# A Strassen-style feed-forward opening put in written order, and one more product beside each table operation of the last state-space quarter

## The chip, the cores and the metric

One core of a Trainium2 chip. The kernel is one launch; its time is the device time of that launch in microseconds (us), here the median of three runs. Engines are called by the profile's names: PE (TensorE products; PEld its weight loads), DVE (VectorE), ACT (ScalarE), POOL (GpSimd) and SP (the engine that issues nearly all DMAs).

## The reference, cut to what matters

One layer of a decoder trunk on x of 1024 tokens by 1024 channels, all in float32:

```python
h = rms_norm(x, mix_norm_g)                      # one projection of h feeds three mixers
y_ssm, y_conv, y_attn = s5(...), short_conv(...), sparse_attention(...)
mixed = sum_b sigmoid(gate_b) * y_b
x = x + mixed @ w_out
h = rms_norm(x, ffn_norm_g)
x = x + (silu(h @ w_gate) * (h @ w_up)) @ w_down   # inner width 2816
```

The s5 mixer is a diagonal complex state-space layer. The kernel computes it in four quarters of its groups.

## The kernel before, in words

Every float32 product is made of three PE products of split operands: each operand x is split into hi (written by ACT, a copy rounded to fp32r) and lo = x - hi (written by DVE, `split`, lines 59 to 62), and hi*hi, hi*lo and lo*hi are added up in PSUM. "A product" below is one of these PE instructions, 128x128 weights by 512 columns; a group that belongs together has 12 of them (4 blocks of the inner dimension by 3).

PSUM has four one-bank accumulators (`acc`) and two two-bank ones (`wide`); SBUF is cut into 44 pages of 128x1024 and 14 half pages. The framework's planner orders the instructions of each engine by the order of the program text and by when it believes operands to be ready; on the chip each engine then runs its list in that order. Within `manual_schedule(engines=...)` the listed engines keep the order of the text among the instructions of that block; what is written before or after the block may still be placed between them.

**State-space quarters.** `s5` loops over q = 0..3 (PE in written order). In each pass the table operations on DVE (`s5_scan` for quarter q, then `s5_tables` for quarter q+1, 25 steps) are followed by `beat()`, which takes a number `F5B` of products from a generator of other work, the filler (`tail`: the rest of the convolution, then the products of two mixers, `mix_plain`). Every 12 products of `mix_plain` end in one DVE instruction (L1166) that empties an accumulator. What is left of the filler after quarter 3 is run by `drain`, then `mix_ssm` follows, whose inputs are the quarters' outputs (`s5_out`, which ends in ACT's L1075, then `s5_back` through memory, then `s5_parts`, a split); its first 12 products end in ACT's L1192.

**The output projection and the feed-forward opening.** `out_rows` computes x + mixed @ w_out by a seven-product Strassen scheme (order `OUT`), 28 steps of four token blocks. The last four steps (p = 4, i = 0..3, the steps 24 to 27) add to the same four accumulators `first[0..3]` that p = 7 has filled; `into` (L1292, DVE) adds an accumulator to a row block of x. `row` normalises a finished block: a sum of squares on ACT (`square_sum`, L219), a square root on ACT (L209), a reciprocal (L210) and a scaling (L215 on DVE or L213 on ACT). `quadrants` transposes normalised blocks on PE, 128x128 at a time (L1373), in fours into a half of a `wide`, from which ACT (L1379) or, for the differences T1, DVE (L1377) takes them; `operand_b` splits them. Of the eight row blocks, 0 to 3 make `half0` (quadrants 11 and 21), 4 to 7 make `half1` (T1 and 22); T2, T3 and T4 are differences made by DVE (L1389).

`ffn_up` is a generator: it fetches weights, makes operands A (`operand`), and then runs groups of 12 products (here called items) in the order of the list `flat`, each preceded by the operand of the item three later. Items 0 to 11 are p = 1 and p = 2 for i = 0..2 and z = 0 (gate), 1 (up); p = 2 adds to the accumulator of p = 1 after ACT has copied it (`p1`, L1520). Items from 12 on need T1, T2, T3, T4 and 22, and for many of them a sum S made by DVE (L1449) before the split. Each `next(up)` in `out_rows` runs the generator to its next `yield`. In the kernel before all engines of this part are ordered by the planner.

Of the kernel before, what the change touches and what calls it, by code (L numbers as in the profile page):

```python
# [11 lines left out]
AF = mybir.ActivationFunctionType  # L12
# [3 lines left out]
P = 128  # L16
# [3 lines left out]
KD = D // P  # L20
# [13 lines left out]
class Trunk:  # L34
# [1069 lines left out]
    def s5(self):  # L1104
        self.yT = []
        tab = self.tab
        for q in range(4):
            bp, cr, bb, ep = tab.pop(q)
            M = self.s5_kernel(q, cr, bb)
            cp = self.s5_carry(cr)  # L1110
            U = self.U[q]
            B = self.s5_inputs(q, bp)
            if q:
                self.s5_back()
            self.F5B = 3.5 if q < 3 else 5
            X = self.s5_scan(q, U, B, ep)
            if q < 3:
                for _ in self.s5_tables(q + 1, tab):
                    self.beat()
            self.fill(self.F5S)  # L1120
            self.s5_out(q, U, M, X, cp)
        self.fill(16)
        self.s5_back()
        self.fill(16)
        self.s5_parts()
# [130 lines left out]
    def out_rows(self):  # L1256
        nc = self.nc
        v = nc.vector
        x2, ss, xn = {}, self.const("ss2", [P, NT]), {}
        self.spill_x = self.dram.tile([S, D], F32, tag="sx", name="sx")  # L1260
        up = self.ffn_up()
        seq, parts = self.out_seq, {}

        def load(t):
            x2[t] = self.page("x2")
            nc.sync.dma_start(x2[t], self.i["x"][0, t * P:(t + 1) * P, :])

        def split(n):
            if n >= len(seq) or n in parts:
                return  # L1270
            p, i = seq[n]
            if n not in self.out_parts:
                self.out_right(n)
            r = self.left[i]
            if p in (1, 2):
                t = r.pop(p)
            else:
                t = self.page("lp", F32R)
                self.split(t[:, :512], t[:, 512:], r["src"].pop(p))
            parts[n] = t, self.out_parts.pop(n)  # L1280

        def mm(ps, n, t):
            p, i = seq[n]
            act, w = parts[n]
            for j, (x, y) in enumerate(((0, 0), (0, 1), (1, 0))):
                nc.tensor.matmul(ps, act[:, x * 512 + t * P:x * 512 + (t + 1) * P], w[:, y * 512:y * 512 + 512],  # L1286
                                 start=i == 0 and j == 0 and p in (1, 5, 2), stop=i == 3 and j == 2,
                                 skip_group_check=True)

        def into(t, c, ps):  # L1290
            o = x2[t][:, c * 512:c * 512 + 512]
            v.scalar_tensor_tensor(o, ps, 0.5, o, op0=OP.mult, op1=OP.add)  # L1292

        def row(t, act):
            self.square_sum(x2[t], ss[:, t:t + 1])
            xn[t] = self.norm_row(x2[t], ss[:, t:t + 1], act)
            nc.sync.dma_start(self.spill_x[t * P:(t + 1) * P, :], x2[t])
            del x2[t]
        INTO = {1: ((0, 0),), 2: ((0, 0),), 5: ((1, 1),), 6: ((0, 1),), 3: ((0, 1),), 7: ((1, 1),), 4: ((1, 0),)}
        for t in range(4):  # L1300
            load(t)
        first = [self.acc() for _ in range(4)]
        second = None
        for n, (p, i) in enumerate(seq[:-4]):
            if i == 0 and p in (5, 2):
                second = []
                for _ in range(2):
                    a = self.wide()
                    second += [a[:, :512], a[:, 512:]]
            if p == 2:  # L1310
                load(4 + i)
            for m in range(n, n + 3):
                split(m)
            for t in range(4):
                ps = (first if p in (1, 6, 7) else second)[t]
                mm(ps, n, t)
                if i == 3:
                    for h, c in INTO[p]:
                        into(4 * h + t, c, ps)
            del parts[n]  # L1320
            if p == 7 and i < 2:
                row(2 * i, 0)
                row(2 * i + 1, 0)
            if p == 7 and i == 0:
                next(up)
        n0 = len(seq) - 4
        for n in range(n0, n0 + 4):
            split(n)
        self.B, half0 = {}, [xn.pop(j) for j in range(4)]
        q = self.quadrants(half0, 0)  # L1330
        for t in range(4):
            for n in range(n0, n0 + 4):
                mm(first[t], n, t)
            into(4 + t, 0, first[t])
            if t == 0:
                q += self.quadrants(half0, 4)
            elif t == 1:
                self.operand_b("11", q[:4])
                next(up)
            elif t == 2:  # L1340
                self.operand_b("21", q[4:])
            if t:
                row(3 + t, t % 2)
        row(7, 0)
        parts.clear()
        next(up)
        half1 = [xn.pop(4 + j) for j in range(4)]
        b11, b21 = q[:4], q[4:]
        t1 = self.quadrants(half1, 0, b11)
        self.operand_b("T1", t1)  # L1350
        next(up)
        b22 = self.quadrants(half1, 4)
        t2 = self.difference(v, b22, t1)
        self.operand_b("T2", t2)
        next(up)
        t3 = self.difference(v, t2, b11)
        self.operand_b("T3", t3)
        next(up)
        t4 = self.difference(v, b21, t2)
        self.operand_b("T4", t4)  # L1360
        self.operand_b("22", b22)
        self.run(up)

    def quadrants(self, xs, k0, less=None):

        nc = self.nc
        r = []
        for k in range(k0, k0 + 4):
            if k % 2 == 0:
                page, two = self.page("bq"), self.wide()  # L1370
            b = two[:, (k % 2) * 512:(k % 2) * 512 + 512]
            for j in range(4):
                nc.tensor.transpose(b[:, j * P:(j + 1) * P], xs[j][:, k * P:(k + 1) * P], self.ident)  # L1373
            o = page[:, (k % 2) * 512:(k % 2) * 512 + 512]
            g = self.gn[:, 8 + k:9 + k]
            if less:
                nc.vector.scalar_tensor_tensor(o, b, g, less[k - k0], op0=OP.mult, op1=OP.subtract)  # L1377
            else:
                nc.scalar.activation(o, b, AF.Identity, scale=g)  # L1379
            r.append(o)  # L1380
        return r

    def difference(self, eng, a, b):
        r = []
# [6 lines left out]
        return r  # L1391

    def operand_b(self, name, src):
        r = []
        for x in src:
            p = self.page("B", F32R)
            self.split(p[:, :512], p[:, 512:], x)
            r.append(p)
        self.B[name] = r


    ORDER = (1, 5, 2, 6, 7, 4, 3)
# [2 lines left out]
    def ffn_up(self):  # L1405
# [3 lines left out]
        gu = self.i["ffn_w_gate_up"][0]  # L1409
        self.spill_a = {p: self.dram.tile([D_FF // 2, HALF], F32, tag=f"sa{p}", name=f"sa{p}") for p in self.ORDER}  # L1410
        N = 3
        flat = [(i, z, p) for i in range(N) for z in range(2) for p in (1, 2)]
        flat += [(i, z, p) for i in range(N) for p in self.ORDER[1:] if p != 2 for z in range(2)]
        flat += [(i, z, p) for i in range(N, NF // 2) for z in range(2) for p in self.ORDER]
        groups = [(i, z, 0) for i in range(N) for z in range(2)]
# [15 lines left out]
        def operand(n):  # L1431
            if n >= len(flat) or flat[n] in ops:
                return
            i, z, p = flat[n]
            g = i, z, int(i >= N or i > 0 and p not in (1, 2))
            if g[2] == 0 and p == 2 and i < N - 2:
                fetch(groups.index(g) + 4)
            elif p == 5:
                fetch(max(groups.index(g) + 2, 2 * N + z))
            lo, hi = raw[g]  # L1440
            a11, a21, a12, a22 = lo[:, :, 0], lo[:, :, 1], hi[:, :, 0], hi[:, :, 1]
            cut = lambda x: x.rearrange("p (k c) -> p k c", k=4)
            if p in (1, 2, 4):
                src = {1: a11, 2: a12, 4: a22}[p]
            else:
                src = cut(self.half("S"))
                x, y, op = {5: (a21, a22, OP.add), 6: (sums.get((i, z, 5)), a11, OP.subtract),
                            7: (a11, a21, OP.subtract), 3: (a12, sums.get((i, z, 6)), OP.subtract)}[p]
                v.tensor_tensor(src, x, y, op=op)  # L1449
                if p in (5, 6):  # L1450
                    sums[i, z, p] = src
            t = self.page("A", F32R)
            self.split(cut(t[:, :512]), cut(t[:, 512:]), src)
            ops[flat[n]] = t
# [33 lines left out]
        yield  # L1488
        for n in range(5):
            operand(n)  # L1490
        yield
        for n, (i, z, p) in enumerate(flat):
            if n in (5, 7, 9, 12):
                yield
            if n == len(flat) - 5:
                self.down = self.ffn_down()
# [290 lines left out]
```

## Time and profile before

| | us |
|---|---|
| median of 3 runs (1753.19 to 1754.08) | 1753.66 |
| profiled execution, its own time | 1753.43 |
| its span in the trace | 1751.5 |
| PE busy in the span | 1728.9 |
| DVE busy | 1202.8 |
| ACT busy | 795.4 |

Busy PE time contains modelled ends of overlapping products, so a gap is read from the start of one product to the start of the next.

### The profile page before, as it was taken

What the parts mean: (1) busy time and instruction counts of PE and PEld (TensorE: products, weight loads), DVE (VectorE), ACT (ScalarE), POOL (GpSimd) and SP (SyncE); (2) the same over time, 40 slices, a digit from 0 to 9 for tenths busy, and PEclk for the clock granted to TensorE, in tenths of its full rate; (3) what the DMA queues carried; (4) which work ended last, traced back from release to release, by engine and by line L of the source; (5) the groups of instructions that cost most, each with busy time, mean ns of one, the idle gap of its engine ahead of it and who ended that gap; (6) DMA issues with size and microseconds to landing.
All of it is one profiled execution on the core that took longest, in us unless ns stands there. A gap on an engine that the chain in (4) does not pass through costs nothing.

```text
span 1751.5 us, 23611 instructions
## 1 busy us (share of the span) xinstructions
PE 1728.9 (99%) x8637; PEld 1433.2 (82%) x8637; DVE 1202.8 (69%) x2414; ACT 795.4 (45%) x1477; POOL 108.8 (6%) x94
## 2 busy tenths in 40 slices
PE   8999999999999999999999999999999999999999
PEld 8987788888888888888788888778888888888887
DVE  6975456667676664684685687798677776687681
ACT  7415566777777842333122244742222332344460
POOL 0000000000000010121000000011122111120000
PEclk9999999999999999999999999999999999999999
DMA  5213422221211125123566224333223332577521
GB/s 173 73 43 101 125 85 67 61 61 46 58 43 47 42 81 145 41 69 97 191 200 200 84 96 133 120 127 127 96 96 109 114 103 78 189 256 259 163 91 48
DMA packets 172664, 189.78 MB, mean 108 GB/s; under 512 B 16937, under 2 KB 129669, under 8 KB 172549
## 3 DMA queue, kind: packets, MB, share of 16 engines
q1 hardware_dynamic: 172517, 188.27, 33.5%
q8 instruction: 68, 1.11, 0.3%
q14 instruction: 47, 0.39, 0.1%
q10 hardware_dynamic: 32, 0.01, 0.0%
HBM read 134.50 MB, written 47.45 MB: 104 GB/s over the span
## 4 chain that ended last, share of the span: by engine, by line
PE 86%; DVE 6%; ACT 4%; issue 1%; DMA 1%; SPq 1%; POOL 0%; POOLq 0%; ACTq 0%; DVEq 0%
PE wide L1517 13%; PE acc L124 12%; PE acc L120 12%; PE acc L122 11%; PE acc L1517 9%; PE acc L1624 6%; PE wide L1624 5%; PE acc L560 3%; PE wide L519 3%; PE acc L1286 2%; PE wide L1286 2%; PE acc L583 2%; PE acc L582 2%; PE wide L257 1%; PE wide L256 1%
## 5 line engine op out<-in xcount | busy, mean ns | idle before, releaser
L120 PE MATMUL acc<-hh,whi 128*128 128x512 f32 x672 | 268.6, 400 | 1.5 <-DVE kl L66 1.5
L122 PE MATMUL acc<-hl,whi 128*128 128x512 f32 x672 | 267.9, 399 | 0.0
L124 PE MATMUL acc<-hh,wlo 128*128 128x512 f32 x672 | 267.4, 398 | 0.0
L1517 PE MATMUL wide<-B,A 128*128 128x512 f32 x1056 | 250.6, 391 | 0.3
L1517 PEld LDWEIGHTS wide<-B,A 128*128 128x128 f32 x1056 | 196.5, 188 | 47.0 <-DVE sg L1530 3.3
L1517 PE MATMUL acc<-B,A 128*128 128x512 f32 x792 | 190.6, 391 | 2.6 <-ACT A L61 1.6
L1517 PEld LDWEIGHTS acc<-B,A 128*128 128x128 f32 x792 | 147.9, 188 | 35.4 <-ACT A L61 2.5
L120 PEld LDWEIGHTS acc<-hh,whi 128*128 128x128 f32 x672 | 126.6, 188 | 22.3 <-issue 2.2
L122 PEld LDWEIGHTS acc<-hl,whi 128*128 128x128 f32 x672 | 126.7, 188 | 19.7 <-issue 0.2
L124 PEld LDWEIGHTS acc<-hh,wlo 128*128 128x128 f32 x672 | 126.8, 189 | 19.4 <-DVE wlo L62 0.4
L61 ACT ACTIVATE A<-S 128x512 fp32r<-128x512 f32 x88 | 54.8, 627 | 164.9 <-DVE S L1449 164.3
L62 DVE TENSOR_TENSOR ptl<-acc,pth 128x512 fp32r<-128x512 f32 (+1 forms) x152 | 93.8, 619 | 50.4 <-ACT pth L61 49.2
L1624 PE MATMUL acc<-wdp,act 128*128 128x512 f32 x528 | 121.5, 389 | 0.1
L524 DVE CUSTOM_DVE_ANT_0 p<-wide,mask 128x640 f32<-128x640 f32 (+7 forms) x128 | 90.1, 704 | 43.2 <-PE wide L519 40.5
L62 DVE TENSOR_TENSOR wlo<-raw,whi 128x1024 fp32r<-128x1024 f32 (+1 forms) x75 | 90.4, 1209 | 39.5 <-ACT whi L61 23.9
L1624 PEld LDWEIGHTS acc<-wdp,act 128*128 128x128 f32 x528 | 99.0, 188 | 21.2 <-DVE wdp L62 0.5
L1473 POOL TENSOR_TENSOR sg<-sg 128x512 f32<-128x512 f32 x44 | 73.9, 1679 | 590.3 <-ACT A L61 512.5
L527 ACT ACTIVATE p<-p,small 128x640 f32<-128x640 f32 (+7 forms) x128 | 93.6, 731 | 37.1 <-DVE small L524 35.1
L120 PE MATMUL acc<-mhi,whi 128*128 128x512 f32 x256 | 100.5, 392 | 1.8 <-DVE m L1166 1.8
L61 ACT ACTIVATE pth<-acc 128x512 fp32r<-128x512 f32 (+1 forms) x152 | 80.9, 534 | 46.0 <-PE acc L560 45.2
L124 PE MATMUL acc<-mhi,wlo 128*128 128x512 f32 x256 | 100.7, 393 | 0.3 <-DVE wlo L62 0.3
L122 PE MATMUL acc<-mlo,whi 128*128 128x512 f32 x256 | 100.5, 393 | 0.0
(397 smaller groups left out, 3246.1 us busy)
## 6 DMA issues: line engine op xcount, KB each, us to landing
raw<-in_ffn_w_gate_up_dram SPq DMA_DIRECT2D x52, 512.0 KB
raw<-in_w_in_dram SPq DMA_DIRECT2D x48, 512.0 KB
sa<-sg SPq DMA_DIRECT2D x77, 256.0 KB
araw<-sa SPq DMA_DIRECT2D x77, 256.0 KB
sg<-tg SPq DMA_DIRECT2D x48, 256.0 KB
gp<-sg SPq DMA_DIRECT2D x24, 512.0 KB
x<-in_x_dram SPq DMA_DIRECT2D x16, 512.0 KB
wd<-in_ffn_w_down_dram SPq DMA_DIRECT2D x11, 512.0 KB
```

The lines of the kernel that those rows point to most:

```text
L61: self.nc.scalar.activation(hi, src, AF.Copy)
L62: self.nc.vector.tensor_tensor(lo, src, hi.bitcast(F32), op=OP.subtract)
L120: self.nc.tensor.matmul(out, hi(k), mh(k), start=start and j == 0, stop=False)
L122: self.nc.tensor.matmul(out, hi(k), ml(k), start=False, stop=False)
L124: self.nc.tensor.matmul(out, lo(k), mh(k), start=False, stop=stop and j == n - 1)
L519: nc.tensor.matmul(ps[:, c * 512:c * 512 + w], self.QS[t][:, h], k[:, k0 + c * w:k0 + c * w + w], start=z == 0, stop=z == 1)
L524: nc.vector.tensor_tensor_reduce(p[:, :n].rearrange("p (c w) -> p c w", c=pieces), v, m.rearrange("p (c w) -> p c w", c=pieces), scale=-1. ...
L527: nc.scalar.activation(p[:, :n], p[:, :n], AF.Exp, scale=-1.0, bias=st[:, hh:hh + 1], accum_out=st[:, 2 + hh:3 + hh])
L1286: nc.tensor.matmul(ps, act[:, x * 512 + t * P:x * 512 + (t + 1) * P], w[:, y * 512:y * 512 + 512], start=i == 0 and j == 0 and p in (1, 5, ...
L1473: e.tensor_tensor(o, x, y, op=op)
L1517: nc.tensor.matmul(ps, x, y, start=p in (1, 5, 6, 7) and k + j == 0, stop=k == 3 and j == 2, skip_group_check=True)
L1624: nc.tensor.matmul(ps, act[:, x * 512 + t * P:x * 512 + (t + 1) * P], w[:, y * 512:y * 512 + 512], start=i == 0 and j == 0 and p in (1, 5, ...
```

## The change

In `s5` the 25 steps of `s5_tables` for the last quarter (made in the pass q = 2) take 4.5 products each in place of 3.5. In `out_rows` everything from the last four steps of the output projection to the split of quadrant 22 stands in one block in which PE, DVE and ACT keep the written order; the transposes of half0 stand among the products of the last four steps, four per step; the sums of squares of blocks 5 and 7 go from ACT to DVE; `quadrants` becomes `flip` (one k at a time, same instructions); the transposes of half1 stand in pairs between items 5 to 8. In `ffn_up` the first 12 items run z innermost, so that p = 2 no longer follows directly on its p = 1, and the generator yields more often.

```diff
             if q < 3:
+                self.F5B = 3.5 if q < 2 else 4.5
                 for _ in self.s5_tables(q + 1, tab):
                     self.beat()
...
-        def row(t, act):
-            self.square_sum(x2[t], ss[:, t:t + 1])
+        def row(t, act, dve=False):
+            if dve:
+                v.tensor_tensor_reduce(self.page("junk"), x2[t], x2[t], scale=1.0, scalar=0.0, op0=OP.mult, op1=OP.add,
+                                       accum_out=ss[:, t:t + 1])
+            else:
+                self.square_sum(x2[t], ss[:, t:t + 1])
...
+        with self.tc.manual_schedule(engines={E.PE, E.DVE, E.Activation}):
+            for s in range(16):
+                t = s // 4
+                mm(first[t], n0 + s % 4, t)
+                if 2 <= s < KD + 2:
+                    self.flip(half0, s - 2, b0)
+                if 3 <= s < KD + 3:
+                    self.operand_b("11" if s < 7 else "21", b0[s - 3:s - 2])
+                if s % 4 == 3:
+                    into(4 + t, 0, first[t])
+                if s in (7, 10, 14):
+                    next(up)
+                elif s == 11:
+                    row(4, 1)
+                elif s == 12:
+                    row(5, 0, True)
+                elif s == 13:
+                    row(6, 0)
+            row(7, 0, True)
+            parts.clear()
+            next(up)
+            next(up)
+            half1 = [xn.pop(4 + j) for j in range(4)]
+            for k in range(4):
+                self.flip(half1, k, b1, b0[k])
+                if k % 2:
+                    next(up)
+            b11, b21, t1 = b0[:4], b0[4:], b1[:4]
+            self.operand_b("T1", t1)
+            for k in range(4, KD):
+                self.flip(half1, k, b1)
+                if k % 2:
+                    next(up)
+            b22 = b1[4:]
+            t2 = self.difference(v, b22, t1)
+            self.operand_b("T2", t2)
+            t3 = self.difference(v, t2, b11)
+            next(up)
+            self.operand_b("T3", t3)
+            t4 = self.difference(v, b21, t2)
+            next(up)
+            self.operand_b("T4", t4)
+            self.operand_b("22", b22)
         self.run(up)
...
-        flat = [(i, z, p) for i in range(N) for z in range(2) for p in (1, 2)]
+        flat = [(i, z, p) for i in range(N) for p in (1, 2) for z in range(2)]
...
         for n in range(5):
             operand(n)
+            if n in (0, 1, 2):
+                yield
         yield
         for n, (i, z, p) in enumerate(flat):
-            if n in (5, 7, 9, 12):
+            if n in (5, 6, 7, 8, 9, 10, 12):
                 yield
```

## Rows read from the trace of the kernel before

**Rows 1.** The page, part 1: busy us (share) and instructions of each engine.

```profile
PE 1728.9 (99%) x8637; PEld 1433.2 (82%) x8637; DVE 1202.8 (69%) x2414; ACT 795.4 (45%) x1477; POOL 108.8 (6%) x94
```

**Rows 2.** Windows: stretch, length, busy of PE, PEld, DVE, ACT, POOL, clock, DMA.

```profile
848.00:857.00 9.00, 9.00 (x39) 7.38 (x38) 8.25 (x19) 0.88 (x1) 0.46 (x1) 0.83 1.00 376
...
1075.00:1104.60 29.60, 29.50 (x143) 23.40 (x142) 21.11 (x36) 22.80 (x42) 0.00 (x0) 1.00 0.80 272
1104.60:1121.70 17.10, 14.91 (x69) 12.00 (x68) 7.08 (x14) 12.46 (x23) 0.00 (x0) 1.00 0.43 146
1121.70:1157.60 35.90, 34.24 (x156) 26.70 (x157) 35.25 (x59) 23.69 (x43) 0.00 (x0) 1.00 0.24 81
1157.60:1240.00 82.40, 82.40 (x365) 68.08 (x364) 71.11 (x94) 24.64 (x41) 19.04 (x12) 1.00 0.36 123
```

**Rows 3.** Timeline of PE, 843 to 852 us: start, us, instruction [idle before <-releaser].

```profile
844.34 0.39 PE L124 MATMUL acc<-mhi,wlo 128*128 128x512 f32 x1
846.53 0.47 PE L120 MATMUL acc<-mhi,whi 128*128 128x512 f32 x1 [1.81 <-DVE m L1166]
...
847.86 0.63 PE L124 MATMUL acc<-mhi,wlo 128*128 128x512 f32 x1
...
850.84 0.50 PE L120 MATMUL acc<-mhi,whi 128*128 128x512 f32 x1
```

**Rows 4.** Timeline of DVE, 832 to 856 us.

```profile
843.06 0.68 DVE L903 TENSOR_TENSOR tt<-lpi,bbi 128x512 f32<-128x512 f32 x1
843.66 1.22 DVE L62 TENSOR_TENSOR wlo<-raw,whi 128x1024 fp32r<-128x1024 f32 x1
...
845.71 0.68 DVE L1166 SCALAR_TENSOR_TENSOR m<-gp,acc 128x512 f32<-128x512 f32 x1
```

**Rows 5.** Timeline of ACT, 895 to 965 us.

```profile
910.54 1.03 ACT L1075 ACTIVATE YN<-wide 128x1024 f32<-128x1024 f32 x1 [18.87 <-PE wide L1072]
...
923.27 2.07 ACT L61 ACTIVATE mhi<-yT 128x1024 fp32r<-128x1024 f32 x1 [10.76 <-DMA yT<-sy]
...
939.34 0.60 ACT L1192 ACTIVATE tgp<-acc 128x512 f32<-128x512 f32 x1 [12.11 <-PE acc L124]
```

**Rows 6.** Timeline of PE, 1085 to 1123 us.

```profile
1086.82 3.00 PE L1286 MATMUL acc<-wop,lp 128*128 128x512 f32 x12
...
1104.65 13.77 PE L1517 MATMUL acc<-B,A 128*128 128x512 f32 x60
1118.26 0.81 PE L1373 MATMUL wide<-ident,xn 128*128 128x128 f32 x6
1120.27 0.44 PE L1373 MATMUL wide<-ident,xn 128*128 128x128 f32 x2 [1.20 <-DVE xn L215]
1121.71 1.49 PE L1517 MATMUL acc<-B,A 128*128 128x512 f32 x5 [1.00 <-ACT A L61]
```

**Rows 7.** Timeline of DVE, 1083 to 1100 us.

```profile
1087.80 0.69 DVE L1292 SCALAR_TENSOR_TENSOR x<-acc,x 128x512 f32<-128x512 f32 x1 [3.23 <-PE acc L1286]
...
1088.60 0.75 DVE L215 TENSOR_SCALAR xn<-x,ss 128x1024 f32<-128x1024 f32 x1
...
1091.68 1.88 DVE L1292 SCALAR_TENSOR_TENSOR x<-acc,x 128x512 f32<-128x512 f32 x3
...
1095.28 0.68 DVE L62 TENSOR_TENSOR lp<-tgp,lp 128x512 fp32r<-128x512 f32 x1
```

**Rows 8.** Timeline of ACT, 1079 to 1165 us.

```profile
1079.72 1.05 ACT L219 ACTIVATE junk<-x 128x1024 f32<-128x1024 f32 x1
...
1080.89 0.29 ACT L209 ACTIVATE ss<-ss,eps 128x1 f32<-128x1 f32 x1
...
1109.63 2.18 ACT L61 ACTIVATE B<-bq 128x512 fp32r<-128x512 f32 x4
```

**Rows 9.** The page, part 5: one of the costliest groups, count | busy, mean ns.

```profile
L62 DVE TENSOR_TENSOR wlo<-raw,whi 128x1024 fp32r<-128x1024 f32 (+1 forms) x75 | 90.4, 1209 | 39.5 <-ACT whi L61 23.9
```

**Rows 10.** Timeline of PE, 1136 to 1162 us.

```profile
1142.27 3.01 PE L1517 MATMUL acc<-B,A 128*128 128x512 f32 x12 [0.69 <-ACT p L1520]
```

More of the change, by code (lines that the diff above doesn't have):

```diff
@@ L1329, in out_rows @@
         self.B, half0 = {}, [xn.pop(j) for j in range(4)]
[L1330 to L1359, printed above, removed]
@@ L1360, in out_rows @@
-        self.operand_b("T4", t4)
-        self.operand_b("22", b22)
+        b0, b1 = [], []
+        E = mybir.EngineType
+        with self.tc.manual_schedule(engines={E.PE, E.DVE, E.Activation}):
[41 more added lines that the diff above has]
+            self.operand_b("22", b22)
@@ L1362, in out_rows, with flip @@
         self.run(up)
-    def quadrants(self, xs, k0, less=None):
+    def flip(self, xs, k, r, less=None):
         nc = self.nc
[L1367 to L1381, printed above, removed]
+        if k % 2 == 0:
+            self.flip_page, self.flip_ps = self.page("bq"), self.wide()
+        w = slice((k % 2) * 512, (k % 2) * 512 + 512)
+        b, o, g = self.flip_ps[:, w], self.flip_page[:, w], self.gn[:, 8 + k:9 + k]
+        for j in range(4):
+            nc.tensor.transpose(b[:, j * P:(j + 1) * P], xs[j][:, k * P:(k + 1) * P], self.ident)
+        if less is not None:
+            nc.vector.scalar_tensor_tensor(o, b, g, less, op0=OP.mult, op1=OP.subtract)
+        else:
+            nc.scalar.activation(o, b, AF.Identity, scale=g)
+        r.append(o)
@@ L1393, in operand_b @@
     def operand_b(self, name, src):
-        r = []
         for x in src:
@@ L1397, in operand_b @@
             self.split(p[:, :512], p[:, 512:], x)
-            r.append(p)
-        self.B[name] = r
+            self.B.setdefault(name, []).append(p)
     ORDER = (1, 5, 2, 6, 7, 4, 3)
```

## The prediction

> **What bounds the kernel now.** I read the shares of busy time first: PE 99% [rows 1]. So a change can only win what PE still waits, and loses whatever new wait it puts on PE. Then the windows, for where PE has gaps: none from 1157.6 to 1240 us (82.40 of 82.40), but 2.2 us in 1104.6 to 1121.7 and 1.7 us in 1121.7 to 1157.6, with DVE at 35.25 of 35.90 there [rows 2]. Last the timelines of PE around both edits, for what ends each gap. "Busy" hides small waits, so I count by starts: one product costs (13.77 - 0.39) / 59 = 0.227 us, one transpose (0.81 - 0.27) / 5 = 0.11 us, 0.27 being what a lone transpose takes to its end [rows 6]. From 1121.71 to item 16 (1157.67, just past the window's end) PE ran 156 instructions, items 5 to 15 (132 products, 29.96) and 24 transposes (2.62): 32.6 us of work in 36.0, so 3.4 us of waits [rows 2, 6]. From item 4's end (1104.65 + 60 x 0.227 = 1118.26) to 1121.71 stand 8 transposes (0.87) and 2.6 us of waits, on the scaling of block 7 and on an ACT split [rows 6].
>
> **The state-space edit.** A step from 844.34 to 846.53 us is a wait of 2.19 - 0.23 = 1.96 us: the 49th product of the mixer needs an accumulator that DVE's L1166 has yet to empty, and L1166 stands behind table operations that are dependent and always ready [rows 3, 4]. After it the granted clock falls: 0.83 on average from 848 to 857 [rows 2], and from 847.86 to 850.84 there are seven steps of 0.426 [rows 3], the lower level, 1.2 GHz; with the one before them, eight products lose 0.2 each, 1.6 us. With 4.5 products a step, the mixer starts and its 13th product comes two to three table steps earlier in the text, so L1166 can follow the eighth table operation, which starts at 843.06 and is over at 843.66 by the pitch of its neighbours [rows 4]. If the 1.22 us weight split still goes ahead, L1166 starts at 844.8 and PE waits till 845.6, 1.0 us; if not, it starts at 843.66 and PE waits nothing. I take 0.5 us left and full clock: 1.96 + 1.6 - 0.5 = 3.1 us won. Bounds: 3.6, and nothing if DVE keeps its order. The 25 x 1 = 25 products come out of what is left after the last quarter (5.7 us). The cover there: from L1075 (910.54) the outputs are split on ACT by 923.27 + 2.07 and on DVE 2.1 later, 927.4; they are needed from the tenth product of a group of 12 that ends at 939.3, so at 938.6 [rows 5]. 11.2 us of cover become 5.5. Cost nothing; 1 us if DVE's backlog eats it. The weights and gate pages that these products ask SP for come up to 5.7 us sooner, into a stretch with a DMA share of 1.00 [rows 2]; each is fetched two or three uses ahead, so I take nothing, and the same 1 us as its bound.
>
> **Opening, stage 1: the last four projection steps.** In the text PE now does all four steps for block 0 first, then block 1. Steps 26 and 27 need splits written ahead of the block, so the planner places them as before: behind four L1292 and the norm of block 3, in a DVE queue that starts with the L1292 that waited 3.23 us for PE (1087.80) and ends with the last lo at 1095.28 + 0.68 = 1095.96 [rows 7]. The four transposes that ran ahead of p = 7's last step go behind: 0.44 less, 1095.5. Before, PE went round this by taking other blocks and transposes. Now step 27's last product for block 0 cannot start before 1095.5, though PE is free for these four steps, 3.2 us of work with the first transposes, from 1086.82 - 0.44 + 12 x 0.227 = 1089.1 on [rows 6]. Left from 1095.5: 37 products (8.4) and 28 transposes (3.1), so item 0 starts at 1107.0 in place of 1104.65: **+2.4**. Bounds: 0, if the planner moves these splits into DVE's 3.2 us hole, and 2.5.
>
> **Stage 2: items 0 to 4.** These are 60 products, 1107.0 to 1120.6 if nothing waits; blocks 4 to 7 are then long normalised, so the 2.6 us of waits before 1121.71 go. What is late next: item 2 adds to item 0's accumulator, which ACT must have copied. PE comes to it at 1107.0 + 24 x 0.227 = 1112.4. ACT's queue ahead of that copy, in written order: the evacuations and splits of half0, paced by PE, whose last transposes end at 1102.9 (behind these ACT still has one evacuation, two splits of B and two of operands, 2.7 with the pitch below and a handover of 0.2 to 0.3: 1105.9), then block 4's sum of squares and root, 1080.89 + 0.29 - 1079.72 = 1.46 [rows 8], to 1107.3; its reciprocal with two handovers, 0.3; block 5's sum on DVE, an operation that the trace before doesn't have: the nearest row, an elementwise one of 1024 columns, is 1.21 [rows 9], I take 1.25 (bounds 0.6, the pitch of a 512-column one, and 1.8, three of these), 1108.9; root 0.35; block 6's sum and root 1.46, 1110.7; reciprocal and scaling 0.3 + 0.75 [rows 7], 1111.8; item 2's lo and the last L1292 on DVE, 0.6 each, the pitch (1.88 - 0.69) / 2 of [rows 7], 1113.0; block 7's sum 1.25, root 0.45, 1114.7; two splits at (2.18 - 0.62) / 3 = 0.52 [rows 8], 1115.7; the copy 0.6: 1116.3. PE waits **3.9 us**. Then 36 products and 8 transposes: item 5 starts at 1125.4 against 1121.71, +3.7 in all. On SP, the x blocks' writes and the weight fetches for i = 2 (four DMAs, asked for with the operands of items 2 and 3, by 1116) move too; the first split of those weights is item 8's, past 1125: hidden, and 1 us if SP holds them back.
>
> **Stage 3: items 5 to 15.** PE ends items 5 to 7 and the 24 transposes at 1125.4 + 8.2 + 2.6 = 1136.2; ACT's evacuations and split, then DVE's lo for item 11, end at 1138.7. In written order DVE then makes T2's differences, T2's lo and T3's differences, 12 x 0.6, to 1146.0; only then item 12's sum (0.6). ACT's split of it and, behind that, the copy of item 9's accumulator, end at 1147.8. Item 11 needs that copy and PE is there at 1136.2 + 3 x 2.72 = 1144.3: **3.5 us**. In the trace before, such a copy held PE 0.69 once [rows 10]. Items 11 and 12 then run to 1153.2; item 13's sum stands behind T3's lo and T4's differences (1153.2), sum and split 1.3: 1.3 us and 0.3 for its lo. Item 15's sum, written after the block, comes behind T4's lo at 1160.3, or behind 22's too: 1.7 us, or 4. Together 6.8 against 3.4 before: +3.4 (bounds 0, if sums float into gaps of DVE's chain, and +5.7). Item 16 starts 3.7 + 3.4 = **7.1 us later** than before; from there PE has no waits to make it up with [rows 2].
>
> **The clock.** After the 1.96 us gap the clock fell [rows 3]; after 1.20 and 1.00 us close together it stayed at 1.00 [rows 2, 6]. A gap of 3.9 us is nearer the first, so I count one fall in stage 2, 1.6 us; in stage 3 much of it would lie in the wait for item 13. The Trainium skill (TensorE: Matmul & The Clock Gate, section "What's actually happening") says that the throttled clock is the default and activity releases it; the 1.96 us gap agrees, the two shorter ones show that not every gap counts. By that rule each of the three long gaps would be followed by a fall, which is a rival below.
>
> **Sum.** 1753.43 (this execution; 0.23 under the median) + 7.1 + 1.6 - 3.1 = **1759.0 us**.
>
> **The rivals.**
> *Written order fits (faster).* The point that decides is item 2 at 1112.4: if ACT's queue has reached the copy of item 0's accumulator by then, no wait comes there, and if item 12's sum is made before 1143, stage 3 has none of its waits either, nor the 3.4 us of before. Then +2.4 - 2.4 - 0.1 at item 5, -3.4 after, -3.1 from the quarter: 1753.4 - 6.6 = 1746.8. For it: gate and up alternate, so a copy has 2.7 us that it hadn't, and the normed blocks wait for nobody. Against it: the sum of ACT's queue, 10.4 us from 1105.9 in which PE has 6.5.
> *It cancels (same).* Stage 3 costs what it cost before, as what is written behind the block fills DVE's gaps, and the clock stays: 1753.4 + 3.7 - 3.1 = 1754.0. For it: DVE before had only 0.65 us idle in that window [rows 2], so its total is the same. Against it: the copy of item 9 is inside the block.
> *The clock falls after each long gap.* Two more falls of 1.6: 1762.2. Against it: no fall at 1121.
> *4.5 does nothing.* DVE runs its chain in the same order, L1166 stays at 845.71: 1759.0 + 3.1 = 1762.1. For it: L1166's place is the planner's, not the text's.
>
> **How the numbers follow.** Forecast 0.33, written order fits 0.24, it cancels 0.27, clock 0.10, 4.5 does nothing 0.06. A difference of 0.2%, 3.5 us, is about what a measurement of this kernel can tell from none. Faster 0.24, same 0.27, slower 0.33 + 0.10 + 0.06 = 0.49. The forecast's own range, with stage 1 at its bounds, the late sum at 2.3 and the clock at 0 to 1.6, is 1755 to 1761.5. The range for all cases is 1747 to 1765: below lies half of the faster case, above a slow clock together with a lost 3.1.
>
> **What would show it.** Right: a PE gap of 1 to 2 us near 1092 ended by DVE's splits; one of 3 to 4 us before item 2, ended by the copy L1520, with ACT's roots waiting for DVE ahead of it; one before item 11, again L1520, with DVE busy on L1389 and L62; and 844 us with a gap under 1 us and no clock under 1. Wrong: items 0 to 11 without a gap, or a T2 to T3 chain on DVE with sums S between; or DVE's lo of step 27 before 1093; or L1166 still behind the ninth table operation.

## The result, and the profile after

The changed kernel takes 1769.87 us (median of 5 runs, 1767.6 to 1772.97), the kernel before 1753.19 beside it: ratio 1.0097, 95% interval 1.0083 to 1.0112, so slower by 0.8 to 1.1%. The forecast was 1759.0 with a range up to 1765: the direction was right (slower had been given a chance of 0.49), the loss was 16.7 us where 5.6 were forecast. The profiled execution took 1771.13 us (span 1769.3), against 1753.43.

First the page's part 1 of the kernel after, which answers to [rows 1]: PE's instructions are the same in number, its busy time is 5.4 us longer, products at a lower clock among it, and most of the loss is waiting.

```profile
PE 1734.3 (98%) x8637; PEld 1435.7 (81%) x8637; DVE 1207.0 (68%) x2419; ACT 792.5 (45%) x1472; POOL 108.7 (6%) x94
```

The windows of the kernel after (columns as in [rows 2]), from the second on cut at the same work as there. The projection runs 0.75 us earlier now, so 1075.00 has become 1074.25. The lengths to compare: 29.60 became 35.15 (up to item 0), 17.10 became 19.80 (items 0 to 4), 35.90 became 46.80 (items 5 to 15); from item 16 on nothing changes, 82.40 and 82.30.

```profile
848.00:857.00 9.00, 9.00 (x41) 7.44 (x41) 8.90 (x21) 0.80 (x1) 0.00 (x0) 1.00 1.04 392
1074.25:1109.40 35.15, 32.43 (x144) 24.39 (x142) 23.37 (x41) 23.86 (x45) 0.00 (x0) 0.95 0.60 210
1109.40:1129.20 19.80, 16.48 (x68) 12.99 (x67) 10.83 (x19) 10.07 (x18) 0.00 (x0) 0.91 0.53 173
1129.20:1176.00 46.80, 36.59 (x160) 27.91 (x159) 34.25 (x55) 21.97 (x40) 0.00 (x0) 0.96 0.17 56
1176.00:1258.30 82.30, 82.30 (x364) 68.17 (x363) 70.48 (x92) 24.79 (x41) 19.13 (x12) 1.00 0.37 123
```

PE's timeline of the kernel after from 840 us on, the rows with a wait of 0.5 us or more in front, and item 11 at 1156.65 (start, us, instruction, [idle before <-releaser]):

```profile
910.85 0.94 PE L1072 MATMUL wide<-X,cp 128*128 128x128 f32 x6 [1.45 <-DVE X L1056]
...
1093.00 1.10 PE L1287 MATMUL acc<-wop,lp 128*128 128x512 f32 x2 [1.66 <-DVE wop L62]
...
1104.79 0.66 PE L1390 MATMUL wide<-ident,xn 128*128 128x128 f32 x4 [0.58 <-ACT bq L1394]
...
1117.47 7.80 PE L1531 MATMUL acc<-B,A 128*128 128x512 f32 x26 [2.47 <-ACT p L1534]
...
1128.83 0.66 PE L1390 MATMUL wide<-ident,xn 128*128 128x128 f32 x4 [0.84 <-DVE bq L1392]
...
1133.53 0.66 PE L1390 MATMUL wide<-ident,xn 128*128 128x128 f32 x4 [0.84 <-DVE bq L1392]
...
1140.29 0.65 PE L1390 MATMUL wide<-ident,xn 128*128 128x128 f32 x4 [2.90 <-ACT bq L1394]
...
1144.92 0.66 PE L1390 MATMUL wide<-ident,xn 128*128 128x128 f32 x4 [0.78 <-ACT bq L1394]
...
1156.08 0.73 PE L1531 MATMUL wide<-B,A 128*128 128x512 f32 x2 [2.30 <-ACT A L61]
1156.65 2.94 PE L1531 MATMUL acc<-B,A 128*128 128x512 f32 x12
...
1163.35 3.29 PE L1531 MATMUL wide<-B,A 128*128 128x512 f32 x12 [1.50 <-ACT A L61]
...
1170.09 0.73 PE L1531 MATMUL acc<-B,A 128*128 128x512 f32 x2 [0.73 <-ACT A L61]
...
1172.50 4.14 PE L1531 MATMUL acc<-B,A 128*128 128x512 f32 x10 [1.15 <-DVE A L62]
```

Three kinds stand here. 1093.00, 1117.47 and the four from 1156.08 on are waits that the forecast named: step 26's split, the copy (L1520 before, L1534 now) ahead of item 2, and the sums behind the T2 to T4 chain. The five on L1390 it did not name: each is the second transpose group of a pair, waiting for the evacuation of the first. 910.85 is new too, in the state-space part. The wait at 844 us [rows 3] is gone.

The clock around three of these waits (windows, same columns): right behind 1093.00, 1117.47 and 1172.50 its mean is about 0.6, part of the stretch at 1.2 and part at 2.4 GHz. Before, the one fall there was stood behind 846.53 [rows 2, 3].

```profile
1093.00:1097.00 4.00, 3.90 (x14) 3.08 (x15) 1.75 (x3) 0.72 (x2) 0.00 (x0) 0.64 0.59 212
1117.40:1121.00 3.60, 3.53 (x9) 2.78 (x10) 1.38 (x3) 2.31 (x4) 0.00 (x0) 0.59 0.77 249
1172.50:1177.00 4.50, 4.50 (x13) 3.56 (x14) 3.36 (x6) 1.67 (x3) 0.00 (x0) 0.62 0.00 0
```

Behind the longest wait of these rows, 2.90 us at 1140.29, it did not fall, nor behind 2.30 at 1156.08 and 1.50 at 1163.35:

```profile
1140.20:1145.00 4.80, 3.93 (x21) 3.14 (x22) 1.82 (x3) 1.93 (x4) 0.00 (x0) 1.00 0.00 0
```

### The profile page after: what moved, and what is told of

Read it like the earlier page. It is cut to its first block, busy times and chain, and to the rows that moved or that the text cites. A ratio compares the mean times of both kernels' runs of the same rounds, so it can differ in the third digit from the quotient of the medians.

```text
span 1769.3 us, 23619 instructions
## 1 busy us (share of the span) xinstructions
PE 1734.3 (98%) x8637; PEld 1435.7 (81%) x8637; DVE 1207.0 (68%) x2419; ACT 792.5 (45%) x1472; POOL 108.7 (6%) x94
## 4 chain that ended last, share of the span: by engine, by line
PE 82%; DVE 9%; ACT 4%; issue 2%; SPq 1%; DMA 1%; ACTq 0%; DVEq 0%
PE wide L1531 12%; PE acc L124 11%; PE acc L120 11%; PE acc L122 11%; PE acc L1531 7%; PE acc L1638 7%; PE wide L1638 5%; PE acc L560 3%; PE wide L519 3%; PE acc L1287 2%; PE wide L1287 2%; DVE A L62 2%; PE acc L583 2%; PE acc L582 2%; PE wide L257 1%
```

## The experiments

To compare runs I mark four points in PE's timeline, which bound three stages: step 24's first product, item 0, item 5, and item 18 (from there to the end every run takes 587.8 to 589.2 us). Each cell is the stage's length in that run's profile less the one of the kernel before (14.63, 17.06 and 41.40 us); "median" is less the median of the kernel before that was measured beside the run. The runs are described below; "and" adds an edit to the row above. In the changed kernel stage 1 also holds eight transposes (0.8 us) that ran ahead of step 24 before.

| run | stage 1 | items 0-4 | items 5-17 | median, us |
|---|---|---|---|---|
| changed kernel | +6.3 | +2.8 | +10.8 | +16.7 |
| own tiles | +4.6 | +2.2 | +4.4 | +8.4 |
| PE alone written | +6.0 | -0.9 | +4.7 | +7.9 |
| own tiles, ACT planned | +5.0 | -2.0 | +4.0 | +4.2 |
| own tiles, PE alone | +3.4 | -0.9 | +3.1 | +4.0 |
| and steps outermost | +2.5 | -0.5 | +2.2 | +2.4 |
| and sums between, splits ahead | +0.3 | -0.5 | +4.6 | +2.0 |
| and item 15's sum ahead | +0.3 | -0.5 | +1.9 | +0.1 |
| and items 16, 17 too | +0.3 | -0.6 | 0.0 | -0.3 |

**The two halves of the change, each alone.** The kernel before with the 4.5 alone:

```
 if q < 3:
+    self.F5B = 3.5 if q < 2 else 4.5
```

> The kernel before with the 4.5 products alone. Theory A (each edit acts alone, read by starts of PE from the two traces): the quarter's edit is worth what PE has won when the output projection starts, 1.5 us: 1751.7, gap at 844 us gone and no clock under 1 there, but a new wait of 1.4 us for X just before the last quarter's output. Rival (the forecast's term): 3.1 us, 1750.1, the new wait belongs to the other edit. Rival: nothing, 1753.2.

Measured 1753.7 against 1754.05, ratio 0.9997 [0.9988, 1.0006]: nothing that can be told from no change. The interval, -2.1 to +1.1 us, leaves out the forecast's 3.1 and not theory A's 1.5. In its profile the wait at 844 is gone, a wait on the last quarter's X has come, and the clock falls at 1121, where it stood at 1.00 before [rows 2]. PE's row and a window of this run:

```profile
910.48 0.71 PE L1072 MATMUL wide<-X,cp 128*128 128x128 f32 x4 [1.45 <-DVE X L1056]
```
```profile
1121.00:1126.00 5.00, 5.00 (x19) 3.87 (x18) 3.13 (x6) 1.23 (x3) 0.00 (x0) 0.66 0.14 52
```

The changed kernel without the 4.5, so the opening alone:

> The changed kernel with 3.5 products as before. Theory A: the opening alone costs the sum of the three stages, 5.5 + 2.8 + 10.8 us less 0.8 that the transposes' move gives ahead of stage 1: 18.3 over before, 1771.5; the gap at 844 us and the lowered clock after it are back. Rival (the edits disturb each other, by DMAs and pages): under 15 or over 22 over before.

Measured 1771.92, ratio 1.0102 [1.0088, 1.0115]. The whole loss, as far as these times can tell, is the opening's.

**Own tiles for the transposes.** Each group of four takes an accumulator tile of its own, in place of half of one for two groups:

```
-    self.flip_page, self.flip_ps = self.page("bq"), self.wide()
+    self.flip_page = self.page("bq")
...
-    b, o, g = self.flip_ps[:, w], ...
+    b, o, g = self.wide()[:, :512], ...
```

> The changed kernel, with a two-bank tile of its own for each k in flip in place of one for two k, so that the odd k's transposes need not wait for the even k's evacuation. Theory A (waits of PE in written order, each with its own cause): the four waits of 0.84, 0.84, 2.90 and 0.78 us among the transposes of half1 go, 5.4 us, of which up to 3 come back before items 11 to 15, since ACT reaches the evacuations no sooner: 1764 to 1767. Rival (the chain of splits and differences on DVE sets item 16 whatever PE does): 1769 to 1770. Rival (PE waits alone): 1764.4 or less.

Measured 1762.42, ratio 1.0043 [1.0028, 1.0059]: 8.4 us over the kernel before where the changed kernel is 16.7 over it, so 8.3 less, and more than expected. In its PE timeline two groups follow one another (x8) without a wait, as in the kernel before (below), and the other waits stay:

```profile
1116.88 5.29 PE L1531 MATMUL acc<-B,A 128*128 128x512 f32 x15 [2.94 <-ACT p L1534]
...
1126.78 1.03 PE L1390 MATMUL wide<-ident,xn 128*128 128x128 f32 x8
...
1149.52 0.73 PE L1531 MATMUL wide<-B,A 128*128 128x512 f32 x2 [2.55 <-ACT A L61]
```

The kernel before has the same two-bank tiles shared by two groups each, and its groups follow one another without a wait. PE, and the ACT row that stands between the two PE rows in time:

```profile
1128.29 1.03 PE L1373 MATMUL wide<-ident,xn 128*128 128x128 f32 x8
...
1130.60 1.03 PE L1373 MATMUL wide<-ident,xn 128*128 128x128 f32 x8
```
```profile
1129.63 1.27 ACT L1379 ACTIVATE bq<-wide,gn 128x512 f32<-128x512 f32 x2
```

The trace does not number the tiles, but this fits a planner that took the groups of the two tiles by turns: first halves, their two evacuations, second halves. So PE's second group into a tile waits until the first half has been read, though it writes the other half. The profile names the evacuation as what ended each wait; whether anything but the order kept for a whole tile asks for it, no run shows. That is 0.84 + 0.84 + 2.90 + 0.78 of the waits above, and part of stage 1 (-1.7).

**Which engine's written order costs.** In the block only PE keeps the written order:

```
-with self.tc.manual_schedule(engines={E.PE, E.DVE, E.Activation}):
+with self.tc.manual_schedule(engines={E.PE}):
```

> The changed kernel with only PE kept in written order in the opening; DVE and ACT planned as in the kernel before. Theory A (ACT and DVE queues in written order make stages 2 and 3): the wait for the copy of item 0's accumulator (2.5 us) and those before items 11 to 16 go, stage 1 stays with its splits and its lowered clock (5.5), and the pairs of transposes keep waits of under 1 us each: 1758 to 1762. Rival (the order of PE itself, transposes among products, costs the time): 1767 or more.

Measured 1761.93, ratio 1.0045 [1.0032, 1.0059], as expected: item 2 waits 0.43 us, and no clock fall follows. The pairs' waits stay (0.84, 0.85, 2.90, 0.84). With own tiles, PE and DVE written, ACT alone planned:

> The changed kernel with own tiles for the transposes, and the written order kept for PE and DVE alone: ACT is planned. Theory (the forecast's stage 2: what holds item 2 is ACT's written queue, the copy behind the norms' roots): against the run with own tiles alone, 1762.4, item 2's wait of 2.9 us falls under 0.6 and the copy before item 11 comes in time: 1759.9 or less. Rival (the DVE's written queue holds it, since the roots wait for its sums): the wait stays over 2 us and the time at 1761.5 or above. What is left over 1756.5, the run with PE alone, is what DVE's written order costs.

Measured 1758.44, ratio 1.0027 [1.0018, 1.0037]: 4 us less than own tiles alone. Item 2 does not wait at all, and the price appears at item 13. PE's timeline:

```profile
1108.05 8.77 PE L1531 MATMUL acc<-B,A 128*128 128x512 f32 x38
1117.16 5.28 PE L1531 MATMUL acc<-B,A 128*128 128x512 f32 x22 [0.34 <-DVE A L62]
...
1151.90 4.87 PE L1531 MATMUL wide<-B,A 128*128 128x512 f32 x12 [3.58 <-ACT A L61]
```

Both mends together, own tiles and PE alone:

> The changed kernel with two edits together: each group of four transposes has an accumulator tile of its own, and only PE keeps the written order in the block, DVE and ACT are planned. Theory (the two causes lie on the path one after the other): PE-only alone left 0.85 + 0.85 + 2.90 + 0.84 = 5.4 us of waits between paired transposes, and these go: 1761.9 - 5.4 = 1756.5, range 1755.5 to 1757.5. The first wait of stage 1 (1.7 us near 1093) and its clock fall stay. Rival (the waits hide behind each other: what the transposes no longer wait, PE waits for item 12's or 13's operands): no better than the better of the two alone, 1760.5 to 1762.

Measured 1757.88, ratio 1.0022 [1.0013, 1.0031], 0.4 above the theory's range: of the 5.4 us that the pairs waited with PE alone written, 4 are won. Some comes back at item 13's third product, whose wait for its lo on DVE grows from 1.61 to 3.35 us. (The expectations of the later runs call it item 14's; the count of products puts it at 13.) With own tiles, the written order thus costs 8.4 us on three engines, 4.2 on PE and DVE and 4.0 on PE alone: ACT's is what cost, DVE's nothing that can be told.

**Stage 1: steps outermost.** PE takes step 24 for all four blocks, then 25 to 27; the four sums and norms follow step 27:

```
-    t = s // 4
-    mm(first[t], n0 + s % 4, t)
+    t = s % 4
+    mm(first[t], n0 + s // 4, t)
```

> The changed kernel (three engines in written order, paired transposes on one tile), with the steps outermost in stage 1 alone. Theory: item 0 starts 3.3 us earlier (no 1.66 us gap at 1093, no clock fall), but the sums and norms of all four blocks now stand together behind the last step and ahead of the copy of item 0's accumulator in ACT's queue: item 2's wait grows from 2.5 to 4 to 5.5. 1769.9 - 3.3 + 1.5 to 3 = 1768 to 1769.6. Rival (the chain ahead of the copy was as long before, only spread): the whole 3.3 us arrive, 1766.6.

That edit alone: 1769.81, ratio 1.0092 [1.0079, 1.0106], no gain. Stage 1 fell from +6.3 to +3.8, and item 2's wait grew from 2.5 to 3.5 us, the way the theory had it, if less than its 4 to 5.5. With own tiles and PE alone:

> As the run before this one, and in stage 1 PE takes step 24 for the four blocks, then 25, 26, 27 (steps outermost, blocks inside); the four sums into x and the four norms follow step 27. Theory (stage 1 pays because block 0 needs step 27's split too early): the 1.7 us gap near 1093 and the clock fall behind it (1.6) go, 1756.5 - 3.3 = 1753.2, range 1752 to 1754.5, so within 0.1% of the kernel before. Rival (the splits are late in any order, since they stand behind the four sums of blocks 0 to 3 in DVE's queue): the gap stays at 1.5 or more and the time at 1756 or above. Second rival: the norms, now all behind the last step, make the four blocks late for their transposes: a gap of over 2 us before half 1's first transpose, 1755 or above.

Measured 1756.24, ratio 1.0014 [1.0005, 1.0023]; 1753.2 was expected, so the theory was too hopeful. The clock no longer falls in stage 1, but PE still waits 1.30 us there, for a sum into x that stands behind four splits on DVE, and item 13's wait for its lo stays, 3.35.

**Stage 3: the place of the sums.** The two calls that write the next items' sums go back behind T2's and T3's splits, where they stood before the change:

```
 self.operand_b("T2", t2)
+next(up)
 t3 = self.difference(v, t2, b11)
-next(up)
 self.operand_b("T3", t3)
+next(up)
 t4 = self.difference(v, b21, t2)
-next(up)
```

> The changed kernel (three engines in written order, paired transposes on one tile) with only the two calls put back behind T2's and T3's splits. Theory (the forecast's stage 3: sums behind the T2 to T4 chain are what PE waits for at items 12 to 15): of the waits 2.30, 1.50, 0.73 and 1.15 us after item 11 some 3 us go, 1769.9 - 3 = 1767, range 1765.5 to 1768. Rival (the pairs of transposes set the pace up to item 11 and DVE's total is the same, so T3's and T4's operands come later by what the sums come earlier): 1769 to 1771.

Alone: 1771.12, ratio 1.01 [1.0085, 1.0116]. The rival is right: nothing gained. On top of the three mends:

> As the run with three edits (own tiles for the transposes, PE alone in written order, steps outermost in stage 1), and the calls that write the next items' sums and splits stand where they stood before the change: behind T2's splits and behind T3's splits, not inside the T2 to T4 chain. Theory (stage 3's remainder is the place of the sums: the split that item 14 waited 3.35 us for stood behind T4's four differences on DVE): that wait and the clock fall behind it go, 1756.2 - 3.3 = 1752.9, range 1751.8 to 1754.2: no difference from the kernel before. Rival (DVE is full there, so T3's or T4's operands come late instead): a wait of 2 us or more moves to the items behind 14 and the time stays at 1755.5 or above.

Measured 1758.25, ratio 1.0028 [1.0017, 1.0039]. The rival again: item 13 no longer waits, item 15 waits 4.4. Then the last steps' splits are also written up to five steps ahead (`n + 5` for `n + 3`):

> As the run before this one, and the splits of the last four projection steps are written up to five steps ahead instead of three. Theory (the 1.3 us that PE waits at step 24's second block is two of these splits' four DVE operations standing between the first and the second sum into x): the four sums then follow one another, the wait goes, 1.0 to 1.3 us less than the run before: 1751.7, range 1750.5 to 1753, which is 0.1% under the kernel before. Rival (the splits are late then, as they follow the sums either way): the wait moves to steps 26 or 27, same time within 0.4.

Measured 1755.88, ratio 1.0011 [1.0002, 1.002]: stage 1's wait is gone (+0.3 left) and the time 2.4 us under the run before; the 1751.7 that was expected is missed, as item 15 still waits 4.4. What item 15 waits for is in DVE's timeline of this run: its sum (L1456, 1153.73) stands behind T4's four differences and eight lo.

```profile
1146.51 2.49 DVE L1398 TENSOR_TENSOR df<-bq,df 128x512 f32<-128x512 f32 x4
1148.91 2.49 DVE L62 TENSOR_TENSOR B<-df,B 128x512 fp32r<-128x512 f32 x4
1151.32 2.49 DVE L62 TENSOR_TENSOR B<-bq,B 128x512 fp32r<-128x512 f32 x4
1153.73 0.68 DVE L1456 TENSOR_TENSOR S<-S,raw 128x512 f32<-128x512 f32 x1
```

So one sum, item 15's, is written ahead of them, and then those of items 15 to 17 (`n + 7` for the last line below):

```
-for m in range(n, n + 4):
+for m in range(n, n + (5 if n == 11 else 4)):
     operand(m)
```

> As the run with all five edits (own tiles for the transposes, PE alone in written order, steps outermost, sums between, splits ahead), and item 15's sum is written one item earlier, ahead of T4's differences. Theory (the 4.4 us that PE waits at item 15 there is one DVE operation, its sum, standing behind four differences and eight lo splits, 7.2 us of DVE's list): the wait and the loss that stays behind it go, 3 to 4.4 us: 1755.9 - 3.5 = 1752.4, range 1751.3 to 1753.5, 0.1% under the kernel before. Rival (DVE's total sets the end of this stage: T4's lo come 1.2 us later and items 16 to 20 wait for them): 1755 or above. Second rival: the profile's place of the loss does not show in the median, because the lowered clock comes and goes between executions: 1754 to 1755.

> As the run with all five edits and item 15's sum ahead, but the sums of items 15, 16 and 17 together are written ahead of T4's differences (the planner of the kernel before put six sums there too). Theory (place, not total: each wait of 3 to 4 us came from one sum written behind T4's chain): item 16's wait of 2.9 us and the clock fall behind it go, 1754.4 - 2.5 = 1751.9, range 1750.8 to 1753, which would be 0.15% under the kernel before. Rival (DVE's total, since T4's and 22's lo now end 1.2 us later still): PE waits for T4's splits at items 16 to 19 instead, 1753.8 or above.

Measured 1754.36, ratio 1.0 [0.9991, 1.0009], and 1753.64, ratio 1.0 [0.9991, 1.0009], both above their theories' ranges. Each time the wait moved on: 2.9 us at item 16 with the one, at item 18 with the three, and there no clock fall followed. PE's timeline and two windows of the second:

```profile
1153.29 5.60 PE L1526 MATMUL wide<-B,A 128*128 128x512 f32 x24
1161.76 8.42 PE L1526 MATMUL wide<-B,A 128*128 128x512 f32 x36 [2.86 <-ACT A L61]
```
```profile
1131.00:1161.00 30.00, 27.89 (x125) 22.70 (x124) 29.93 (x51) 17.52 (x31) 0.00 (x0) 1.00 0.32 106
1161.00:1170.00 9.00, 8.24 (x36) 6.87 (x37) 8.01 (x15) 3.12 (x5) 0.00 (x0) 1.00 0.46 143
```

From the order without these two edits (+4.6) to the last one (0.0) the place of the sums was worth 4.6 us of the profile, the clock behind the wait at item 15 included (its mean was 0.57 from 1154 to 1162 us); against the row "and steps outermost" it was worth 2.2. What is left is as much as before the change, in one wait in place of several. DVE is busy for 29.93 of the 30 us from 1131 to 1161, up to the end of that wait, and no order tried goes below it, which speaks for DVE's total as the bound there; no run took work off DVE in this stage, and the sum of item 18 was not moved ahead as well, so that stays argued.

**The 4.5 once more.** Three of these kernels without it:

> As the run with all three edits (own tiles, PE only, steps outermost), without the 4.5: the opening by itself, mended. Theory (the state-space edit is worth nothing in the end, as its own run had it): the same within 0.6 us as that run. Rival (its 1.5 us at the output projection arrive when no gap behind it lowers the clock again): 1.3 to 1.7 us slower than that run.

> As the run with all five edits (own tiles, PE alone, steps outermost, sums between, splits ahead), without the 4.5. Theory (the state-space edit trades its first wait for another): the same time within 0.7 us, so 1751.7, range 1750.5 to 1753. Rival (it is worth the 1.5 us seen at the output projection): 1753 to 1753.5.

> The same without the 4.5 of the state-space quarter. Theory (its first wait is traded for the second, whose price is about the same): within 0.7 us of that run. Rival (its 1.2 us show once nothing behind eats them): 1.0 to 1.6 us slower.

Measured 1757.08 [1.0011, 1.0029] beside 1756.24 with it, 1755.89 [1.0003, 1.0021] beside 1755.88, and 1752.83 [0.9987, 1.0004] beside 1753.64: the intervals overlap each time, and the sign changes; the first is 0.84 us slower without it, outside the theory's 0.6 and short of the rival's 1.3, the second is the theory's, and the third is 0.81 faster, just outside the theory's 0.7 and away from the rival. All six profiles agree with one another: with the 4.5 the 1.45 us wait on X is there, without it the 1.96 us wait at 844 is. Behind that one the clock fell in the kernel before, in the opening alone and in the last of these three, but not in the first two; the window of the second is:

```profile
846.00:857.00 11.00, 9.20 (x44) 7.40 (x44) 10.97 (x24) 1.06 (x1) 0.00 (x0) 1.00 0.95 347
```

The best version, with all of this, ties with the kernel before and does not beat it. How much the clock blurs this shows when the executions are sorted by their mean granted clock: at 1.000 the last run without the 4.5 takes 1751.5 us (mean of 5), the same with it 1752.9 (5) and the kernel before 1753.2 (8). That was sorted after the fact, and no run tests it.

## Why the prediction was right in direction and wrong in size

Nearly all that the forecast listed as signs of being right came in kind: the gap near 1092, the copy ahead of item 2, the wait before item 11, the free 844. The time left the range because the list of waits was not complete. By its own steps. DVE's and ACT's timelines of the changed kernel carry most of it; DVE first:

```profile
843.84 0.67 DVE L1167 SCALAR_TENSOR_TENSOR m<-gp,acc 128x512 f32<-128x512 f32 x1
...
908.87 1.23 DVE L1171 TENSOR_TENSOR m<-m,gp 128x1024 f32<-128x1024 f32 x1
910.11 0.68 DVE L1056 TENSOR_TENSOR X<-m,m 64x508 f32<-64x508 f32 x1
...
1090.47 1.88 DVE L1293 SCALAR_TENSOR_TENSOR x<-acc,x 128x512 f32<-128x512 f32 x3
1092.27 0.68 DVE L62 TENSOR_TENSOR wop<-wo,wop 128x512 fp32r<-128x512 f32 x1
...
1152.28 2.49 DVE L1403 TENSOR_TENSOR df<-df,bq 128x512 f32<-128x512 f32 x4
1154.69 0.68 DVE L1461 TENSOR_TENSOR S<-raw 128x512 f32<-128x512 f32 x1
```

then ACT:

```profile
1112.02 0.62 ACT L61 ACTIVATE A<-raw 128x512 fp32r<-128x512 f32 x1
1115.60 0.29 ACT L209 ACTIVATE ss<-ss,eps 128x1 f32<-128x1 f32 x1 [2.96 <-DVE ss L1297]
1115.80 1.13 ACT L61 ACTIVATE A<-raw 128x512 fp32r<-128x512 f32 x2
1116.84 1.06 ACT L1534 ACTIVATE p<-acc 128x512 f32<-128x512 f32 x2
...
1137.48 2.17 ACT L61 ACTIVATE B<-bq 128x512 fp32r<-128x512 f32 x4
1139.56 0.67 ACT L1394 ACTIVATE bq<-wide,gn 128x512 f32<-128x512 f32 x1
...
1155.40 0.63 ACT L61 ACTIVATE A<-S 128x512 fp32r<-128x512 f32 x1 [4.35 <-DVE S L1461]
1155.94 0.58 ACT L1534 ACTIVATE p<-acc 128x512 f32<-128x512 f32 x1
```

- **The state-space edit, -3.1: failed.** The 844 us wait went, all of it, where 0.5 us was to stay (L1167 at 843.84, L1166 at 845.71 before [rows 4]). What failed is "Cost nothing; 1 us if DVE's backlog eats it" for the moved 25 products. In the last quarter three of mix 2's sums (L1171) now stand on DVE ahead of the last X, where one stood before; PE waits 1.45 us for X, in every run with the 4.5 and in none without. By this profile the edit is worth 0.75 us where the projection starts; by the other five pairs of profiles with and without it, from -1.2 to +1.5, as the clock fell or not behind the other wait; in time, nothing that can be measured. The step looked at the splits behind the quarter and not at the scan inside it.
- **Stage 1, +2.4: the term held, two others were missing beside it.** Step 26's split ran behind the four L1293, as said, and PE waited 1.66 us for it. By the forecast's own measure, item 0's start, the loss was 4.75 + 0.75 = 5.5 us: a clock fall (the window at 0.64 cost 0.36 x 4.0 = 1.4), 1.7 for the paired transposes by the own-tiles run, and 2.4 for this wait, shorter ones on the splits beside it and the transposes put behind. That it is just the 2.4 forecast is partly luck: PE stood at step 26, not at step 27.
- **Stage 2, a 3.9 us wait: the right wait, 2.5 measured.** The chain is the one that was written out: block 7's root waits 2.96 us for DVE's sum, two splits follow, then the copy, and item 2 starts at 1117.47, 1.2 us after the 1116.3 forecast; PE came to it later still, 1109.40 + 5.45 = 1114.85 where 1112.4 was forecast. With ACT planned the wait is gone. The sum was 1.21 + 0.08 us, 1.25 was taken.
- **Stage 3, +3.4: the step that failed.** What it worked out did come: item 12's sum at 1154.69 behind T3's differences, its split, the copy behind that at 1155.94, item 11 at 1156.65. (PE's wait ends with the split, since two of item 12's products, which are written behind the block, stand ahead of item 11 in PE's list.) By starts, items 11, 13 and 15 lost 2.6, 1.7 and 0.9 + 1.4 us, 6.6 where 6.8 was forecast; the sum is nearer than its parts, 3.5, 1.6 and 1.7. What failed is that the 24 transposes were put at their work alone, 2.6 us: 0.84, 2.90 and 0.78 us of waits between the halves of a tile here, and one 0.84 in stage 2. The 2.90 is the worst case: the second group waits for an evacuation (1139.56) that ACT's written list has behind four splits. I had counted the transposes by the pitch of [rows 6], where the planner had put other tiles between, and not looked at which tile each group writes.
- **The clock, one fall: wrong, three in the profiled execution.** It fell behind 1.66, 2.47 and 1.15 us (the last behind three waits within 10 us). The other executions had other shares of it: at a mean granted clock of 0.999 the changed kernel took 1767.6 us, at 0.996 1772.97. The Trainium skill (TensorE: Matmul & The Clock Gate, section "What's actually happening") says that the throttled clock is the default and activity releases it. The forecast made of it a rival in which a fall follows each long gap, and that rival came nearest in time with 1762.2. The runs bear it out in part: no fall followed 2.90 and 2.30 us in this same profile, nor 2.86 us at item 18.

The misses make the size: 7.7 us for the pairs (by starts, the second groups of half 1 came 1.0, 1.0, 3.1 and 0.9 late, and 1.7 in stage 1), some 3.2 for two more falls at the forecast's 1.6 each, 2.4 for the state-space edit (3.1 less 0.75), less 1.4 at item 2: 1759.0 + 11.9 = 1770.9, and the profiled execution had 1771.13. That it closes so well is partly luck, as the terms were read in different ways. "Written order fits" and "it cancels" fell with the first two waits.

## What to carry to other kernels

When a planner's order is replaced by a written one, list for each instruction which tile it writes and who has to read it first: two groups that share a tile were free as long as something stood between them, and cost some 8 us side by side. Bind by hand only the engine whose order matters; here PE's alone cost half of what PE's, DVE's and ACT's together did, and with own tiles the other half was ACT's. And a wait taken off a full engine travelled here, from item 2 to 13, from 13 to 15, to 16, to 18: price the engine's sum over the stage before its order.

## What was not expected of the hardware

The same waits did not always lower the clock: 1.20 and 1.00 us before item 5 left it at 1.00 in the kernel before [rows 2, 6] and brought it to 0.66 in the run with the 4.5 alone; 1.96 us at 844 lowered it there, in the opening alone and in the last run without the 4.5, and not in the other two without it. The 2.90 us between the transposes left it at 1.00 in the changed kernel and brought it down in the run with the sums between alone, where the same wait stands at 1139.90:

```profile
1139.90:1144.60 4.70, 4.70 (x16) 3.79 (x17) 1.03 (x2) 1.21 (x2) 0.00 (x0) 0.64 0.00 0
```

So some 1.6 us per fall can be counted, but not whether one comes.
